# A two-layer diffusion backbone on one core: four weight tiles of layer 1's v placed in attention's operand slots, row statistics put off by two products, and another order of VectorE at the last scores

## The chip, the cores and the metric

The kernel runs on one core of a Trainium2 chip. The metric is the device time of one execution in microseconds. A run is given as the median of several executions. Besides, one execution is taken with the hardware profiler; it has its own time and a trace of every instruction.

A core has five engines with one instruction queue each: TensorE (PE in the profile, with its weight loads as PEld), VectorE (DVE), ScalarE (ACT), GpSimd (POOL) and SyncE (SP). An engine executes its queue in order. If an instruction waits, everything behind it on that engine waits too.

## The reference

The model has two layers over 512 latent tokens (x) and 256 context tokens (ctx), each 1024 wide. Layer 0 mixes tokens by retention with four heads. Layer 1 is a chunked gMLP; of it the part that the change touches is the projection to v and its normalisation over a row:

```
hx = rmsnorm(x, norm_g[i]) * (1 + scale_x) + shift_x
hc = rmsnorm(ctx, norm_g[i]) * (1 + scale_c) + shift_c

# layer 0, retention, per head: scores = (q @ k.T) * decay, o = scores @ v
o = o * lax.rsqrt(jnp.mean(o * o, axis=-1, keepdims=True) + NORM_EPS)
out_x = (o * silu(z)) @ w_out
x = x + gate_x * out_x

# layer 1, gMLP
u = h @ w_in[:, :2048]
v = h @ w_in[:, 2048:4096]
z = h @ w_in[:, 4096:]
v = v - mean(v)
v = v * rsqrt(mean(v * v) + NORM_EPS) * vnorm_g
mixed = w_s @ vg + b_s            # inside chunks of 128 tokens, 8 groups
y = u * mixed
x = x + gate_x * ((y * silu(z)) @ w_out)
return rmsnorm(x, final_g)
```

## The kernel before, in words

**Two halves of every number.** All data are 32-bit floats. Each operand of a product is kept as two halves: a high one, rounded to the type fp32r, and the low rest. `split` (L132) makes them: ScalarE copies the source into the high half (a cast), VectorE subtracts the high half from the source. `mm3` (L126) adds three matmuls for each term: low by high, high by low, high by high. So one weight tile costs one ScalarE cast and one VectorE subtraction, each 128 x 1024, and it waits for a free slot.

**Fewer products.** A large product of 2 by 2 blocks is done in seven products instead of eight, in the order `PAIRED` (L152): B11, B21, T1, T2, B22, T3, T4. The weight of a product whose name begins with B is one block of the matrix. That of a T product is a difference of two blocks (a raw sum: VectorE subtracts one 128 x 1024 raw block from another). `WITH` (L151) names the operand made of the tokens: A11 for B11, A12 for B21, S1 for T1, S2 for T2, S4 for B22, S3 for T3 and A22 for T4. `Product.run` (L369) runs one product of 24 matmuls into a bank of PSUM and then combines: `snap` (L350) is a ScalarE copy of the bank into SBUF, `plus` (L354) a VectorE addition of a bank to an earlier copy. There are eight PSUM banks, six with the tag ps and two with the tag tm. For a block of columns B21 uses a tm bank (y), and T1 takes another (z). T1 of the next block can start only when a plus has read such a bank to its end; T4 goes into the same bank x as B11, T2 and T3 after the plus of T3 in that block.

**The stream of weights.** `Stream` (L155) holds the list of all weight tiles in the order of their use. `pump` (L182) sends loads of raw blocks on SP's queue whenever a slot for a raw is free. `upto(n)` (L196) makes the tiles up to number n: it takes the raw sum if one is needed, takes a slot, and splits. At its end it makes the sum of the next tile ahead of its split. `sum(n)` (L214) does only the sum. `get(ahead=2)` (L239) returns the next tile and prepares two more behind it. The tiles lie in a ring of four slots, hl0 to hl3 (`hl_tile`, L110), unless an item names a slot of its own by `place_at` (L287). Layer 1's v has four blocks of columns, taken in two pairs: 0 and 1, then 2 and 3. For the first pair the item list (L290 to L297) puts the two tiles of B11 into oA22 and oS2; all others go to the ring.

**Attention.** The slots oA11, oA12, oA22 and oS1 to oS4 have 8 KB for each partition. While a head runs, its v lies in oA11, oS1 and oS2 (`load_v`, L903), z in oA12, and the transposed output og in oS3 and oS4; oA22 is free. `attend` (L962) has six steps, three for each half (hf) of the queries, and two further turns (LAG = 2). In a turn i, `score` (L973) issues the score products of step i, then VectorE multiplies by the decay (tile pf) and `split` gives ph on ScalarE and pl on VectorE. `pv` (L992) issues the products with v of step i - 2. After the last of a half, `finish` (L1005) normalises the rows: ScalarE squares and takes a square root, VectorE a reciprocal and two multiplications that give gt. `flip` (L1018) turns gt with eight transposes on TensorE and splits the result into og. Beside these, each turn takes pieces of other work off generators: qs and vs (loads and splits of the next head), wo (the weight tiles of this head's output product).

**Between the layers.** `project_out` (L1052) multiplies og with the output weights for each half of the tokens and four weight tiles (c), and adds the result to acc on VectorE (128 x 256 at a time). In the last head it calls hooks: `prepare` (L1192) at (hf, c) = (0, 2), which opens layer 1's loads and calls `Q.upto(Q.at + 1 + 2 + 2)`, and `first_half` (L1141) for each (hf, c). That starts the norm of layer 1 for the first half of the tokens: `by_tokens` (L1104) transposes acc and squares it on ScalarE, `inverse` (L1120) and `rms` (L1127) give the inverse root (tile sums, spread out by TensorE to rs), `scaled` (L1135) multiplies f by rs and scales it, `op` and `keep` (L320, L323) split the result into a slot. The second half of the tokens and the operands S1 to S4 and A22 are made in `second_half` (L1161), a generator, one piece after each of the first products of v.

**Layer 1's v.** The loop at L1215 to L1224 runs all products of a pair by name and block. `v1_done` (L1203) is called when a part of v is finished: two row statistics (bns, 128 x 256 each on VectorE, `bn_stats`), and a spill of v to DRAM by GpSimd's DMA queue. After both pairs the statistics are aggregated, and the loop over u, z and the output products follows.

**Who sets the order.** `Queue` (L38) wraps an engine. With `kept` an engine's instructions keep the order of the text; `fence()` (L47) keeps later instructions of that engine behind the last one issued so far, without a semaphore. Where neither is set, the tile scheduler orders the instructions of an engine within the dependences of tiles and slots. All rows of the profile say L54, because the wrapper issues every instruction there; rows are told apart by the program's names.

Of the kernel before, what the change touches and what calls it, by code (L numbers as in the profile page):

```python
# [18 lines left out]
HEADS = 4  # L19
# [7 lines left out]
HS = 256  # L27
# [40 lines left out]
def hybrid_kernel(ctx, tc, xT_d, cT_d, cv_d, sv_d, rows_d, ada0_d, adag_d, w_d, rope_d, dec_d, ws_d, id_d, out_d):  # L68
    nc = tc.nc
    pe, act, dve, sp = (Queue(tc, e) for e in (nc.tensor, nc.scalar, nc.vector, nc.sync))  # L70
# [11 lines left out]
    def st(shape, tag, dt=F32, bufs=1, name=None):  # L82
        return sb.tile(shape, dt, tag=tag, name=name or tag, bufs=bufs)
# [34 lines left out]
    def t2(name, shape=(P, 512), dt=F32):  # L118
        return st(list(shape), "t2", dt, bufs=T2, name=name)
# [124 lines left out]
    Q = Stream()  # L244
# [42 lines left out]
    def place_at(tag):  # L287
        return lambda: st([P, 2, 1024], tag, F32R, name="hl_e")

    V1_SLOTS = W + ["dec", "rope", "g0", "g2", "g3"]  # L290
    for a, b in ((0, 1), (2, 3)):
        for name in PAIRED:
            for cb in (a, b):
                Q.item(("v1", cb), name, place_at(("oA22", "oS2")[cb]) if (a, name) == (0, "B11") else None)
        for u in ("11", "21", "12", "22"):
            for cb in (a, b):
                Q.load((("v1", cb), u), V1_SLOTS, 2, parts_of(("v1", cb), u))  # L297

# [528 lines left out]
    def aside(work):  # L827

        act.pinned = dve.pinned = True
        r = next(work, None)  # L830
        act.pinned = dve.pinned = False
        return r
# [53 lines left out]
    wos = {}  # L886
# [75 lines left out]
    def attend(h, qs, vs):  # L962
        q, k, kc = qk.pop(h)
        v, z = vv.pop(h)
        dt = dts[h]
        og = [st([P, 2, 4, HS], tag, F32R, name="og") for tag in ("oS3", "oS4")]
        steps = [(hf, j) for hf in range(2) for j in range(0, NK, 2)]
        ph, po, pend = {}, {}, []

        def key(j):  # L970
            return (k[j // 2], j % 2) if j < NT else (kc, j - NT)

        def score(hf, j):  # L973

            p = pt(tag="tm")
            for o in range(2):
                src, jj = key(j + 1 - o)
                for m in range(2):
                    l = (src[:, 0, m, jj * P:jj * P + P], src[:, 1, m, jj * P:jj * P + P])
                    mm3(p[:, o * HS:o * HS + HS], l, (q[hf][:, 0, m, :], q[hf][:, 1, m, :]), m == 0, m == 1)  # L980
            j1 = j + 1
            s0 = hf * HS - P * j1 + P * (NT - 1) if j < NT else XW + hf * HS - P * (j1 - NT) + P * (NC_T - 1)
            base = dt[:, s0:s0 + HS]
            both = bass.AP(base.tensor, base.offset, [base.ap[0], (P, 2), (1, HS)])
            two = lambda x: x.rearrange("p (o t) -> p o t", o=2)
            a = t2("pf")
            dve.scalar_tensor_tensor(two(a), two(p), 1.0 / 16.0, both, ALU.mult, ALU.mult)
            hl = t2("ph", dt=F32R), t2("pl", dt=F32R)
            split(hl, a)
            ph[hf, j] = hl  # L990

        def pv(hf, j):  # L992
            if j == 0:
                po[hf] = [pt(), pt()]
            h, l = ph.pop((hf, j))
            src = v[j // 2]
            for jj in range(2):
                for t in range(2):
                    o = (1 - jj) * HS + t * P
                    mm3(po[hf][t], (h[:, o:o + P], l[:, o:o + P]), (src[:, 0, jj, :], src[:, 1, jj, :]),  # L1000
                        j + jj == 0, j + jj == NK - 1)
            if j == NK - 2:
                finish(hf)

        def finish(hf):  # L1005
            ss = st([P, 2], "ss", bufs=2)
            for t in range(2):
                act.activation(t2("junk"), po[hf][t], AF.Square, accum_out=ss[:, t:t + 1])
            act.activation(ss, ss, AF.Sqrt, bias=eps, scale=1.0 / 512)
            dve.reciprocal(ss, ss)  # L1010
            gts = []
            for t in range(2):
                g = t2("gt")
                dve.scalar_tensor_tensor(g, po[hf][t], ss[:, t:t + 1], z[:, 2 * hf + t, :], ALU.mult, ALU.mult)
                gts.append(g)
            pend.append((hf, gts))

        def flip():  # L1018
            hf, gts = pend.pop(0)
            for fp in range(2):  # L1020
                pq = pt()
                for b in range(2):
                    for t in range(2):
                        o = b * HS + t * P
                        pe.transpose(pq[:, o:o + P], gts[t][:, (2 * fp + b) * P:(2 * fp + b) * P + P], ident)
                src = pq.rearrange("p (b t) -> p b t", b=2)
                split((og[hf][:, 0, 2 * fp:2 * fp + 2, :], og[hf][:, 1, 2 * fp:2 * fp + 2, :]), src)

        LAG = 2
        wo = load_wo(h)  # L1030
        for i in range(len(steps) + LAG):
            if i < len(steps):
                score(*steps[i])
            if i >= LAG:
                pv(*steps[i - LAG])
            aside(qs)
            if i > 4:
                aside(vs)
            if i == len(steps):
                flip()  # L1040
            if (h, i) == (0, 2):
                sp.pinned = True
                for c in range(4):
                    load(acc[:, 2 * c:2 * c + 2, :], xT_d[:, 2 * c:2 * c + 2, :])
                sp.pinned = False
            if i < 5:
                aside(wo)
            if i in (3, 5, 6):
                step()
        return og, flip  # L1050

    def project_out(ws, og, flip, parts, then=None, between=None, prepare=None):  # L1052
        for hf in range(2):
            sl = slice(hf * HS, hf * HS + HS)
            for c in range(4):
                w = ws[c]
                if (hf, c) == (0, 2):
                    flip()
                    if prepare:
                        prepare()  # L1060
                for work in parts:
                    aside(work)
                if then is None and hf == 1 and c < 3:
                    step()
                if between:
                    between(hf, c)
                for mi in range(2):
                    m = 2 * c + mi
                    p = pt((P, HS))
                    for kk in range(4):  # L1070
                        o = kk * 256 + mi * P
                        mm3(p, (w[:, 0, o:o + P], w[:, 1, o:o + P]), (og[hf][:, 0, kk, :], og[hf][:, 1, kk, :]), kk == 0, kk == 3)
                    dve.scalar_tensor_tensor(acc[:, m, sl], p, gate0[:, m:m + 1], acc[:, m, sl], ALU.mult, ALU.add)
                    if then:
                        then(hf, m)
# [37 lines left out]
    def residual():  # L1113
        while flipped:
            i, pq = flipped.pop(0)
            xs = t2("xs")
            act.copy(xs, pq)
            spill(x1_d[i], xs)
# [73 lines left out]
    def prepare():  # L1192
        Q.stage = 2
        Q.free += V1_SLOTS[len(W):] + [w for w in W if w not in Q.free]
        Q.pump()
        Q.upto(Q.at + 1 + 2 + 2)

    project_out(wos.pop(HEADS - 1), og, flip, (), then=half_sum, between=first_half, prepare=prepare)


    bns = st([P, NT, 8, 6], "bns")

    def v1_done(cb):  # L1203
        def done(name, c):
            if name == "21":
                t = t2("snap")
                act.copy(t, c)
                c = t
            th, nh = int(name[0]) - 1, int(name[1]) - 1
            for t in range(2):  # L1210
                dve.bn_stats(bns[:, 2 * th + t, 2 * cb + nh, :], c[:, t * HS:t * HS + HS])
            spill(vt_d[2 * cb + nh][:, 2 * th:2 * th + 2, :], c.rearrange("p (t n) -> p t n", t=2))
        return done

    chain = second_half()  # L1215
    for a, b in ((0, 1), (2, 3)):
        prods = {q: Product(tokens, v1_done(q)) for q in (a, b)}
        for name in PAIRED:
            for q in (a, b):
                prods[q].run(name, Q.get())  # L1220
                if a == 0 and (q == 0 and name in ("B11", "B21", "T1", "T2", "B22") or (name, q) == ("B11", 1)):
                    next(chain)
            if (a, name) == (0, "B21"):
                residual()  # L1224
    bsb = st([P, D], "rope", name="bsb")
    load(bsb, rows_d[2:3, :].partition_broadcast(P))
    wsT = st([P, D], "dec", name="wsT")
# [265 lines left out]
```

## Time and profile before

| | |
|---|---|
| median of 3 runs | 893.61 us (890.0 to 894.43) |
| the profiled execution, its own time | 895.05 us |
| its span, from first to last instruction | 893.3 us |
| mean granted TensorE clock | 0.998 |
| VectorE: the splits of weight tiles (hl), 195 | 236.6 us, 1220 ns each |
| VectorE: raw sums, 92 | 111.7 us, 1219 ns each |
| ScalarE: casts of weight tiles, 195 | 203.8 us, 1051 ns each |
| DMA | 153.81 MB, mean 172 GB/s |

The profiled execution has 1.75 us around its span, and is 1.44 us above the median. Busy time counts an instruction from its start to its end, and for TensorE the ends are modelled, so neighbours can overlap: the time that TensorE loses is better read from the distance of two starts than from the busy share. In a row of the timeline the first number is the start in us from the span's start, the second the stretch that the group covers, then the engine, the line, the operation, the tiles it writes and reads, the shape and the number of instructions; in brackets stands the idle time before it and what ended that. A row of the waits gives engine, tile, the releaser, the total in us, how often, and the longest. A row of the windows gives a stretch, its length, the busy time of each engine with the number of instructions, the granted clock and the share of the DMA engines.

### The profile page before, as it was taken

The page shows a single profiled execution, that of the slowest core. Times are in us where ns is not written, and L with a number is a line of the kernel's source. Part 1 is how long each engine was busy: PE and PEld are TensorE (multiplying, and loading weights), DVE is VectorE, ACT ScalarE, POOL GpSimd, SP SyncE. Part 2 cuts the span into 40 slices and gives each one's busy share as a digit, 9 for nine tenths or more (in the row PEclk, how much of TensorE's full clock was granted, in tenths as well). Part 3 has the DMA queues.
Part 4 walks back from the last instruction along what each step waited for, and adds up shares of the span by engine and source line. Part 5 has one row for each costly group of instructions (what it writes and reads, how often), then busy time and mean ns, then how long its engine had stood idle before and what let it go on. Part 6 is the DMA issues. An engine that isn't in the chain of part 4 may idle for free.

```text
span 893.3 us, 16943 instructions
## 1 busy us (share of the span) xinstructions
PE 878.2 (98%) x6884; PEld 835.9 (94%) x6884; DVE 712.8 (80%) x996; ACT 461.9 (52%) x717; POOL 51.5 (6%) x88
## 2 busy tenths in 40 slices
PE   8999999999999999999999999989999999999997
PEld 6899999999999999998989999989999899899986
DVE  2689967699779876878677558999898578688995
ACT  5464644443545435636265449744666446356434
POOL 0001201002101101000000001010000000000000
PEclk9999999999999999999999999999999999999999
DMA  9933967457577458847354512455335135036112
GB/s 337 403 126 107 298 221 261 141 180 230 191 231 243 152 161 326 282 130 251 128 158 150 164 48 79 156 179 189 131 121 172 62 119 189 24 119 212 56 64 95
DMA packets 75486, 153.81 MB, mean 172 GB/s; under 512 B 7696, under 2 KB 34448, under 8 KB 75408
## 3 DMA queue, kind: packets, MB, share of 16 engines
q1 hardware_dynamic: 68544, 130.69, 44.8%
q0 software_dynamic: 6720, 22.03, 6.5%
q8 instruction: 54, 0.88, 0.4%
q14 instruction: 24, 0.20, 0.1%
q10 hardware_dynamic: 144, 0.01, 0.0%
HBM read 128.58 MB, written 24.12 MB: 171 GB/s over the span
## 4 chain that ended last, share of the span: by engine, by line
PE 86%; DVE 7%; ACT 3%; DMA 2%; issue 1%; SPq 1%; DVEq 0%; ACTq 0%
PE pst L54 86%; DVE hl L54 2%; DVE f L54 1%; DMA xq<-in_xT_dram 1%; DMA raw<-in_w_dram 1%; ACT junk L54 1%; DVE oS L54 1%; SPq L54 1%; DVE snap L54 0%; ACT hl L54 0%; DVE pf L54 0%; DVE pl L54 0%; DVE o L54 0%; DVE bns L54 0%; ACT L54 0%
## 5 line engine op out<-in xcount | busy, mean ns | idle before, releaser
L54 DVE TENSOR_TENSOR hl<-raw,hl 128x1024 fp32r<-128x1024 f32 x195 | 236.6, 1220 | 76.0 <-ACT hl L54 75.9
L54 ACT CAST hl<-raw 128x1024 fp32r<-128x1024 f32 x195 | 203.8, 1051 | 138.5 <-PE pst L54 63.4
L54 PE MATMUL pst<-hl,oS 128*128 128x256 f32 x1152 | 135.5, 278 | 0.0
L54 PEld LDWEIGHTS pst<-hl,oS 128*128 128x128 f32 x1152 | 134.0, 188 | 0.8 <-ACT snap L54 0.8
L54 PE MATMUL pst<-oS,hl 128*128 128x256 f32 x1104 | 133.3, 279 | 0.7 <-ACT oS L54 0.5
L54 PEld LDWEIGHTS pst<-oS,hl 128*128 128x128 f32 x1104 | 129.9, 188 | 2.3 <-ACT oS L54 1.0
L54 PE MATMUL pst<-oA,hl 128*128 128x256 f32 x936 | 117.2, 281 | 0.2
L54 PEld LDWEIGHTS pst<-oA,hl 128*128 128x128 f32 x936 | 111.8, 189 | 2.5 <-DVE rope_b L54 0.8
L54 DVE TENSOR_TENSOR raw<-raw 128x1024 f32<-128x1024 f32 x92 | 111.7, 1219 | 1.0 <-DMA raw<-in_w_dram 0.4
L54 ACT COPY snap<-pst 128x512 f32<-128x512 f32 x92 | 53.9, 586 | 102.1 <-PE pst L54 101.6
L54 PE MATMUL pst<-hl,oA 128*128 128x256 f32 x816 | 100.0, 282 | 2.7 <-DVE snap L54 2.7
L54 PEld LDWEIGHTS pst<-hl,oA 128*128 128x128 f32 x816 | 97.7, 191 | 2.9 <-issue 2.8
L54 PE MATMUL pst<-og,hl 128*128 128x256 f32 x768 | 92.5, 281 | 0.0
L54 PEld LDWEIGHTS pst<-og,hl 128*128 128x128 f32 x768 | 90.5, 189 | 1.0 <-issue 0.5
L54 PE MATMUL pst<-v,ph 128*128 128x512 f32 x192 | 60.1, 395 | 0.0
L54 PE MATMUL pst<-hl,ya 128*128 128x512 f32 (+1 forms) x246 | 59.2, 386 | 0.0
L54 PEld LDWEIGHTS pst<-hl,ya 128*128 128x128 f32 x246 | 45.3, 188 | 9.5
L54 DVE TENSOR_TENSOR snap<-pst,snap 128x512 f32<-128x512 f32 x69 | 47.2, 685 | 4.9 <-PE pst L54 4.6
L54 ACT CAST ph<-pf 128x512 fp32r<-128x512 f32 x24 | 14.9, 622 | 66.9 <-DVE pf L54 66.5
L54 PE MATMUL pst<-hl,hc 128*128 128x256 f32 x384 | 47.4, 280 | 0.0
L54 PEld LDWEIGHTS pst<-hl,hc 128*128 128x128 f32 x384 | 46.0, 189 | 0.0
L54 PEld LDWEIGHTS pst<-v,ph 128*128 128x128 f32 x192 | 36.2, 188 | 7.3
(177 smaller groups left out, 1001.1 us busy)
## 6 DMA issues: line engine op xcount, KB each, us to landing
raw<-in_w_dram SPq DMA_DIRECT2D x224, 256.0 KB, 4.1
bg<-in_adag_dram SPq DMA_DIRECT2D x32, 512.0 KB, 4.4
ada_w<-in_ada_dram SPq DMA_DIRECT2D x16, 512.0 KB, 9.1
raw<-in_w_dram SPq DMA_DIRECT2D x16, 512.0 KB, 4.2
bg<-in_dec_dram SPq DMA_DIRECT2D x12, 512.0 KB, 4.4
v<-snap POOLq DMA_DIRECT2D x16, 256.0 KB, 5.0
z<-snap POOLq DMA_DIRECT2D x16, 256.0 KB, 4.7
v<-v SPq DMA_DIRECT2D x8, 512.0 KB, 4.0
```

The costliest lines, as they stand in the source:

```text
L54: made = op(*args, **kw)
```

## The change

It has four parts.

1. The tiles of B11 for blocks 0 and 1 go to oS1 and oS2, and those of B21 to oA22 and oS3. Before, B11's went to oA22 and oS2, and B21's into the ring.
2. `prepare` makes the tiles of layer 1 up to B21's (`FIRST_V1 + 4`). A new hook `turned` calls `first_half` and, at (hf, c) = (1, 2) and (1, 3), makes the two tiles of T1 as well, which go into the ring. `get` makes two tiles ahead as before.
3. The row statistics of a finished part are put in a list and issued when more than two parts are waiting there, that is some products later; what is left is issued after the loop. The spill stays where it was. At T1 of block 1, the raw sums of items 12 and 13, the tiles of T4 for blocks 0 and 1, are issued early.
4. In `attend`, `finish` of the first half issues only ScalarE's squares and root; the reciprocal and the two multiplications (`gated`) wait in a list. In the next turn VectorE issues the score's pf first, then a fence, and the split's pl and `gated` come behind. In that turn and the one before, the pieces of other work are taken at another place of the text.

```
@@ -287,11 +287,13 @@
+    FIRST_V1 = len(Q.items)
     V1_SLOTS = W + ["dec", "rope", "g0", "g2", "g3"]
     for a, b in ((0, 1), (2, 3)):
         for name in PAIRED:
             for cb in (a, b):
-                Q.item(("v1", cb), name, place_at(("oA22", "oS2")[cb]) if (a, name) == (0, "B11") else None)
+                home = {"B11": ("oS1", "oS2"), "B21": ("oA22", "oS3")}.get(name) if a == 0 else None
+                Q.item(("v1", cb), name, place_at(home[cb]) if home else None)
@@ -965,7 +967,7 @@ attend
-        ph, po, pend = {}, {}, []
+        ph, po, pend, due = {}, {}, [], []
@@ -985,6 +987,8 @@ score
             dve.scalar_tensor_tensor(two(a), two(p), 1.0 / 16.0, both, ALU.mult, ALU.mult)
+            if due:
+                dve.fence()
             hl = t2("ph", dt=F32R), t2("pl", dt=F32R)
             split(hl, a)
@@ -1007,6 +1011,11 @@ finish
             act.activation(ss, ss, AF.Sqrt, bias=eps, scale=1.0 / 512)
+            due.append(lambda: gated(hf, ss))
+            if hf == 1:
+                due.pop(0)()
+
+        def gated(hf, ss):
             dve.reciprocal(ss, ss)
             gts = []
@@ -1031,8 +1040,14 @@ attend
             if i < len(steps):
                 score(*steps[i])
+            if due:
+                due.pop(0)()
+                aside(qs)
+                aside(wo)
             if i >= LAG:
                 pv(*steps[i - LAG])
+            if due:
+                continue
             aside(qs)
@@ -1193,9 +1208,14 @@ prepare
-        Q.upto(Q.at + 1 + 2 + 2)
-
-    project_out(wos.pop(HEADS - 1), og, flip, (), then=half_sum, between=first_half, prepare=prepare)
+        Q.upto(FIRST_V1 + 4)
+
+    def turned(hf, c):
+        first_half(hf, c)
+        if hf == 1 and c >= 2:
+            Q.upto(FIRST_V1 + 3 + c)
+
+    project_out(wos.pop(HEADS - 1), og, flip, (), then=half_sum, between=turned, prepare=prepare)
@@ -1207,21 +1227,34 @@ v1_done
-            for t in range(2):
-                dve.bn_stats(bns[:, 2 * th + t, 2 * cb + nh, :], c[:, t * HS:t * HS + HS])
+            stats.append((th, 2 * cb + nh, c))
             spill(vt_d[2 * cb + nh][:, 2 * th:2 * th + 2, :], c.rearrange("p (t n) -> p t n", t=2))
         return done
+
+    stats = []
+
+    def statistics(n):
+        while len(stats) > n:
+            th, cb, c = stats.pop(0)
+            for t in range(2):
+                dve.bn_stats(bns[:, 2 * th + t, cb, :], c[:, t * HS:t * HS + HS])
@@ the loop over v's products
             for q in (a, b):
-                prods[q].run(name, Q.get())
+                w = Q.get()
+                if (a, name, q) == (0, "T1", 1):
+                    for n in (12, 13):
+                        Q.sum(FIRST_V1 + n)
+                prods[q].run(name, w)
+                statistics(2)
                 if a == 0 and (q == 0 and name in ("B11", "B21", "T1", "T2", "B22") or (name, q) == ("B11", 1)):
                     next(chain)
             if (a, name) == (0, "B21"):
                 residual()
+    statistics(0)
```

## The prediction, made before the changed kernel ran

> **What bounds the kernel now.** I read the page first, then TensorE's waits, then its timeline at each wait, then VectorE's timeline at the same places.
>
> ```profile
> span 893.3 us, 16943 instructions
> PE 878.2 (98%) x6884; PEld 835.9 (94%) x6884; DVE 712.8 (80%) x996; ACT 461.9 (52%) x717; POOL 51.5 (6%) x88
> PE 86%; DVE 7%; ACT 3%; DMA 2%; issue 1%; SPq 1%; DVEq 0%; ACTq 0%
> ...
> PE pst L54 <- DVE snap L54: 2.7, 1, 2.7
> PE pst L54 <- DVE pl L54: 1.5, 3, 0.7
> ```
>
> TensorE is the bound: busy 98%, 86% of the chain that ended last. The change removes no matmul, so it can only close holes in TensorE's queue. The two waits on VectorE are such holes: one for a snap add, three for the low half of a score (pl). A hole's true size is read from starts, because the modelled ends overlap. First the three places where the transposes of gt precede the last products of a head (LAG puts them so), beside an undisturbed set of the same eight transposes:
>
> ```profile
> 364.12 1.03 PE L54 MATMUL pst<-ident,gt 128*128 128x128 f32 x8
> 365.48 0.50 PE L54 MATMUL pst<-v,pl 128*128 128x512 f32 x1 [0.33 <-DVE pl L54]
> ...
> 414.14 1.04 PE L54 MATMUL pst<-ident,gt 128*128 128x128 f32 x8
> 415.61 0.50 PE L54 MATMUL pst<-v,pl 128*128 128x512 f32 x1 [0.43 <-DVE pl L54]
> ...
> 465.38 1.03 PE L54 MATMUL pst<-ident,gt 128*128 128x128 f32 x8
> 467.13 0.51 PE L54 MATMUL pst<-v,pl 128*128 128x512 f32 x1 [0.71 <-DVE pl L54]
> ...
> 475.45 1.03 PE L54 MATMUL pst<-ident,gt 128*128 128x128 f32 x8
> 476.24 17.21 PE L54 MATMUL pst<-og,hl 128*128 128x256 f32 x144
> ```
>
> Undisturbed, the next work starts 0.79 us after the first transpose. Here it starts 1.36, 1.47 and 1.75 us after. The losses are 0.57, 0.68 and 0.96, together 2.2 us. The fourth head shows none.
>
> Second, the end of layer 1's first pair of v blocks. The names: B11, B21, T1, T2, B22, T3, T4 each run for blocks 0 and 1, 24 matmuls a product.
>
> ```profile
> 542.36 0.38 PE L54 MATMUL pst<-ident,acc 128*128 128x128 f32 x2
> 542.94 1.16 PE L54 MATMUL pst<-ident,acc 128*128 128x128 f32 x6 [0.19 <-DVE acc L54]
> 543.85 2.98 PE L54 MATMUL pst<-og,hl 128*128 128x256 f32 x24
> ...
> 553.29 0.70 PE L54 MATMUL pst<-ident,sums 128*128 128x128 f32 x4
> 553.75 5.70 PE L54 MATMUL pst<-hl,oA 128*128 128x256 f32 x48
> 559.29 21.92 PE L54 MATMUL pst<-hl,oS 128*128 128x256 f32 x192
> 583.88 6.29 PE L54 MATMUL pst<-hl,oA 128*128 128x256 f32 x39 [2.67 <-DVE snap L54]
> ...
> 601.90 2.32 PE L54 MATMUL pst<-hl,oS 128*128 128x256 f32 x19
> ```
>
> 192 matmuls are eight products: 2.74 us each. T4 of block 0 starts at 583.88 after 2.67 us of nothing. The second pair's T1 (first with oS1 again) starts at 601.90: six products later, which at 2.74 would be 16.4 us; it took 18.0. The clock tells where the other 1.6 us went:
>
> ```profile
> 581.00:584.00 3.00, 0.34 (x3) 0.17 (x3) 3.00 (x6) 1.88 (x2) 0.05 (x1) 1.00 0.80 255
> 584.00:585.00 1.00, 1.00 (x10) 1.00 (x11) 1.00 (x4) 0.21 (x1) 0.92 (x2) 1.00 0.89 279
> 586.00:587.00 1.00, 1.00 (x6) 1.00 (x6) 1.00 (x4) 0.00 (x0) 0.00 (x0) 0.50 0.87 311
> 587.00:588.00 1.00, 1.00 (x6) 1.00 (x6) 0.90 (x1) 0.00 (x0) 0.00 (x0) 0.50 1.01 393
> ```
>
> The columns after the stretch are its length, the busy time of PE, PEld, DVE, ACT and POOL, then PEclk. Two microseconds after the hole TensorE gets half its clock, and runs 6 matmuls a microsecond where it ran 10. So the hole costs 2.7 + 1.6 us. [...]
>
> **The change, part by part.**
>
> *Last scores first.* In the scheduled order VectorE now has, at the last score of each head, pf, (reciprocal), pl, and only then gt. Before, pf stood behind the reciprocal, which waits for ScalarE's square root:
>
> ```profile
> 461.04 0.17 DVE L54 RECIPROCAL ss<-ss 128x2 f32<-128x2 f32 x1 [2.30 <-ACT ss L54]
> 461.24 1.41 DVE L54 SCALAR_TENSOR_TENSOR gt<-pst,ss,z 128x512 f32<-128x512 f32 x2
> ...
> 464.30 0.68 DVE L54 SCALAR_TENSOR_TENSOR pf<-pst,dt 128x512 f32<-128x512 f32 x1
> ...
> 466.39 0.68 DVE L54 TENSOR_TENSOR pl<-pf,ph 128x512 fp32r<-128x512 f32 x1
> ```
>
> ```profile
> L54 ACT CAST ph<-pf 128x512 fp32r<-128x512 f32 x24 | 14.9, 622 | 66.9 <-DVE pf L54 66.5
> ```
>
> pf falls into those idle 2.30 us. ScalarE casts ph right after the square root, 0.62 us by its group; pl ends near 462.4 instead of 467.1, four microseconds before it is wanted. What is late next is gt: 1.41 us behind pl gives 463.8, wanted by the transposes at 465.38; 1.5 us are left. The same sums hold in the other heads. The skipped asides are made up in the next turn, so no work is added. Gain: 2.2 us. Bounds: 0 if something else ends at the same moment, 2.2.
>
> *Four tiles in attention's slots.* The tiles of B11 and B21 go to oS1, oS2, oA22 and oS3 instead of two there and two in the ring of four. The ring is free sooner, so T1's two splits move before the stage, and the work behind them moves up. No instruction is added. The waits that are added: the cast into oS1 waits on ScalarE for the last product that reads v's second tile, and ahead of it nothing but behind it stand the two og casts for the output product. By the order of ScalarE they come some 0.6 us later than before; VectorE's og halves with them end about 0.6 us before TensorE wants them. The cast into oS3 waits until the first half of the output product is through, and behind it stand the squares of acc: 0.1 us, covered by 24 matmuls. Cost 0; from 0 to 0.5 us if the cover is thinner.
>
> *What VectorE's queue gives.* These are its rows at both ends and the price of each kind:
>
> ```profile
> 542.40 1.65 DVE L54 SCALAR_TENSOR_TENSOR acc<-pst,gate,acc 128x256 f32<-128x256 f32 x4
> 543.97 0.47 DVE L54 SCALAR_TENSOR_TENSOR f<-acc,gs,f 128x256 f32<-128x256 f32 x1
> ...
> 554.43 1.23 DVE L54 TENSOR_TENSOR f<-f,rs 128x1024 f32<-128x1024 f32 x1
> ...
> 579.53 0.68 DVE L54 TENSOR_TENSOR snap<-pst,snap 128x512 f32<-128x512 f32 x1
> 580.13 1.21 DVE L54 TENSOR_TENSOR hl<-raw,hl 128x1024 fp32r<-128x1024 f32 x1
> 581.26 0.74 DVE L54 BATCH_NORM_STATS2 bns<-snap 128x6 f32<-128x256 f32 x2
> 581.93 1.20 DVE L54 TENSOR_TENSOR raw<-raw 128x1024 f32<-128x1024 f32 x1
> 583.05 1.28 DVE L54 TENSOR_TENSOR snap<-pst,snap 128x512 f32<-128x512 f32 x2
> ```
>
> Start to start: snap 0.60, a 1024-wide split 1.13, a pair of bns 0.67, a raw sum 1.12, a 256-wide step about 0.4.
>
> Step 1. acc of the transposes at 542.36: two of the four acc now run before it, because no ring split stands in front. The transposes need 0.79 again instead of 1.49: TensorE is 0.7 us earlier.
>
> Step 2. VectorE then goes without pause to f times rs: one A11 and one A12 split, three ring splits, three raw sums, six 256-wide steps and three tiny ones: 2 x 1.13 + 3 x 1.13 + 3 x 1.12 + 6 x 0.4 + 0.3 = 11.7 us. It starts at 543.2 (0.8 earlier than the row at 543.97), so f times rs comes at 554.9, half a microsecond later than now. TensorE meets two new holes of about 0.4 and 0.9 us: at the transposes of sums (the reciprocal stands behind a raw sum) and at T1 of block 0, whose bank is freed by an add that comes 4.5 us after f times rs (two splits, four 256-wide steps and the add: 2.26 + 1.6 + 0.6). T1 starts at 559.5 instead of 559.29: step 1's gain is used up.
>
> Step 3. From f times rs to T4 took 583.88 - 554.43 = 29.45 us. In the new order that stretch has one split less (T2's two went ahead, T4's second came in), one raw sum less and one pair of bns less: 1.13 + 1.12 + 0.67 = 2.92. T4 can start at 554.9 + 26.5 = 581.4. TensorE itself is there at 559.5 + 8 x 2.74 = 581.4. The hole is gone, 2.5 us earlier, and with it the half clock.
>
> Step 4. The bns put off come later. From there to the add that frees T1's bank in the second pair VectorE has six splits, five raw sums, five pairs of bns and two adds: 6.8 + 5.6 + 3.35 + 1.2 = 16.95, that is 598.3; TensorE alone would be there at 597.8. So T1 starts at 598.3 against 601.90, 3.6 us earlier, the next one 3.5. After that VectorE gains room as it does now.
>
> The weights of layer 1's u are now requested ahead of v's last ones on SP's queue; those have over 10 us until their sums. Cost 0.
>
> Sum: 2.2 + 3.5 = 5.7 us. Span 893.3 becomes 887.6; the profiled execution's 895.05 becomes 889.35. That execution is 1.4 above the median of the runs shown, 893.61; less 5.7 this is 887.9. I say 888.0.
>
> **Rivals.**
>
> *The hole moves* (25%). If steps 2 and 4 are worse by a microsecond each, VectorE is the bound from T1 to T1 and 2 of the 3.5 are lost: gain 3.7, 889.9. For it: VectorE has no pause there now. Against: 2.9 us of work did move ahead.
>
> *The half clock has another cause* (7%) and stays. TensorE would lose 1.6 between T4 and T1, of which VectorE's bound at 598.3 hides 0.5: gain 4.6, 889.0.
>
> *Everything closes* (13%). No new holes in step 2: 0.7 us more in front, and up to 1 us in step 4. Gain 7.4, 886.2.
>
> *Slower* (4%). A cast that waits in ScalarE's queue holds all behind it; one does so now:
>
> ```profile
> 464.16 1.06 ACT L54 CAST hl_e<-raw 128x1024 fp32r<-128x1024 f32 x1 [1.69 <-DMA raw<-in_w_dram]
> ```
>
> In the new order the cast into oS1 stands before og. Beyond its cover of 0.6 us each microsecond is TensorE's, and from about 2 us the clock halves as it did after 2.67: 1.6 more. It must be 4.7 us late to eat the gain (4.7 - 0.6 + 1.6 = 5.7), and 9.1 to give 898.1, 0.5% slower. Nothing in the rows makes it wait longer than for its product.
>
> *The change does not act* (5%): the order is met but the waits stay; 893.
>
> **How the numbers follow.** The forecast has 46%. 0.5% is 4.5 us, which is about what a measurement of this kernel can tell from no change; the runs shown spread over 4.4. Faster by more: the forecast, everything, and about half of the second rival: 62%. Within: most of the first rival, the rest of the second, the fifth: 34%. Slower: 4%. Range: the first rival's 889.9 and everything's 886.2, each widened by 1.5 for the spread of a median: 884.7 to 891.6.
>
> **What would show it.** Right: no wait for pl and none for snap in TensorE's waits; PEclk 1.00 from 560 to 620; pf right after a head's last score; small holes, under 1 us, at sums and T1. Wrong: a hole over 2 us near 558 or 596; og casts that TensorE waits for; a stretch of half clock.

## The result, and the profile after

The changed kernel takes 888.82 us in the median of 13 runs (888.38 to 891.14); the kernel before takes 893.34 us in 13 runs beside it (889.68 to 895.34). The medians lie 4.5 us apart. The comparison of the runs, which is not the quotient of the medians, gives the ratio 0.996, 3.6 us less, with a 95% interval of 0.9947 to 0.9973: 2.4 to 4.7 us less. The profiled execution took 888.54 us; its span is 886.8 us, 6.5 shorter than that of before.

The page of the changed kernel with the chain by engine, and below it one row of TensorE's waits (releaser, total in us, times, longest):

```profile
span 886.8 us, 16946 instructions
PE 876.3 (99%) x6884; PEld 835.0 (94%) x6884; DVE 712.5 (80%) x996; ACT 461.5 (52%) x717; POOL 51.5 (6%) x88
...
PE 91%; DVE 4%; ACT 3%; DMA 1%; issue 1%; SPq 0%; DVEq 0%
```

```profile
PE pst L54 <- DVE snap L54: 0.6, 2, 0.4
```

No row for pl is left among the waits, and snap's 2.7 has become 0.6 in two pieces. No engine does less work: VectorE is busy 712.5 us instead of 712.8. TensorE's share of the chain rises from 86% to 91%.

TensorE's timeline at the places that the prediction showed of before:

```profile
363.30 1.03 PE L54 MATMUL pst<-ident,gt 128*128 128x128 f32 x8
364.09 0.47 PE L54 MATMUL pst<-v,pl 128*128 128x512 f32 x1
...
412.70 1.03 PE L54 MATMUL pst<-ident,gt 128*128 128x128 f32 x8
413.50 0.48 PE L54 MATMUL pst<-v,pl 128*128 128x512 f32 x1
...
463.09 1.03 PE L54 MATMUL pst<-ident,gt 128*128 128x128 f32 x8
463.88 0.48 PE L54 MATMUL pst<-v,pl 128*128 128x512 f32 x1
...
539.08 1.04 PE L54 MATMUL pst<-ident,acc 128*128 128x128 f32 x8
539.88 3.07 PE L54 MATMUL pst<-og,hl 128*128 128x256 f32 x24
...
549.44 0.71 PE L54 MATMUL pst<-ident,sums 128*128 128x128 f32 x4
549.90 6.00 PE L54 MATMUL pst<-hl_e,oA 128*128 128x256 f32 x48
556.16 22.05 PE L54 MATMUL pst<-hl,oS 128*128 128x256 f32 x192 [0.26 <-DVE snap L54]
578.22 16.59 PE L54 MATMUL pst<-hl,oA 128*128 128x256 f32 x144
595.17 5.04 PE L54 MATMUL pst<-hl,oS 128*128 128x256 f32 x41 [0.36 <-DVE snap L54]
```

Each set of transposes is now followed after 0.79 us, the undisturbed distance. T4 (578.22) comes without a wait. The distance of these starts from those of before is a running account, in us:

```
                                        before   after    ahead by   step
first head's transposes of gt           364.12   363.30     0.82
work behind the third head's            467.13   463.88     3.25     +2.43
work behind the transposes of acc       543.85   539.88     3.97     +0.72
work behind the transposes of sums      553.75   549.90     3.85     -0.12
T1 of block 0                           559.29   556.16     3.13     -0.72
T4 of block 0                           583.88   578.22     5.66     +2.53
T1 of block 2                           601.90   595.17     6.73     +1.07
end of the span                         893.3    886.8      6.5      -0.2
```

The first 0.82 us stand ahead of every place that was changed, so they are a difference between two executions (at 230 us the changed kernel is 1.0 us ahead already); the last part on the hardware says which. Of the 2.43 us, 2.21 are the three waits for pl; the other 0.2 lies in the products between the heads.

What moved is seen on VectorE. Here are the same 35 us of TensorE's work in both kernels (stretch, its length, busy time of PE, PEld, DVE, ACT, POOL), first of before, then of after, 3.25 us earlier:

```profile
505.00:515.00 10.00, 10.00 (x55) 8.58 (x54) 5.83 (x8) 5.24 (x10) 0.00 (x0) 1.00 0.87 269
515.00:525.00 10.00, 10.00 (x75) 9.26 (x74) 5.98 (x11) 3.88 (x9) 0.00 (x0) 1.00 0.26 83
525.00:540.00 15.00, 14.75 (x129) 14.51 (x128) 8.93 (x15) 8.09 (x21) 2.18 (x4) 1.00 0.15 54
```

```profile
501.75:511.75 10.00, 10.00 (x55) 8.58 (x54) 7.12 (x10) 5.34 (x10) 0.00 (x0) 1.00 0.82 263
511.75:521.75 10.00, 10.00 (x74) 9.26 (x74) 8.37 (x13) 4.53 (x9) 0.00 (x0) 1.00 0.24 79
521.75:536.75 15.00, 14.75 (x129) 14.51 (x127) 10.69 (x17) 9.55 (x23) 2.17 (x4) 1.00 0.19 71
```

VectorE does 26.18 us of work there instead of 20.74. Most of these 5.4 us are splits and raw sums of v's first tiles (four instructions more, of 1.22 us each), which before stood in the crowded stretch behind. From f times rs to T4 that stretch has no pause of more than 0.1 us on VectorE in either kernel; it only begins with less to do.

### The profile page after: what moved, and what is told of

It reads as the page before. It is cut to its first block, busy times and chain, and to the rows that moved or that the text cites. A ratio compares the mean times of both kernels' runs of the same rounds, so it can differ in the third digit from the quotient of the medians.

```text
span 886.8 us, 16946 instructions
## 1 busy us (share of the span) xinstructions
PE 876.3 (99%) x6884; PEld 835.0 (94%) x6884; DVE 712.5 (80%) x996; ACT 461.5 (52%) x717; POOL 51.5 (6%) x88
## 4 chain that ended last, share of the span: by engine, by line
PE 91%; DVE 4%; ACT 3%; DMA 1%; issue 1%; SPq 0%; DVEq 0%
PE pst L54 91%; DVE hl L54 1%; DMA xq<-in_xT_dram 1%; ACT f L54 1%; ACT junk L54 1%; DVE raw L54 1%; SPq L54 0%; DVE f L54 0%; ACT hl L54 0%; ACT oA L54 0%; DVE o L54 0%; ACT xs L54 0%; DVE oS L54 0%; DVE xq L54 0%; DVE bns L54 0%
## 5 line engine op out<-in xcount | busy, mean ns | idle before, releaser
L54 ACT CAST hl<-raw 128x1024 fp32r<-128x1024 f32 x193 | 201.7, 1050 | 141.7 <-PE pst L54 66.3
L54 PE MATMUL pst<-hl,oA 128*128 128x256 f32 x768 | 92.2, 278 | 0.0
L54 PEld LDWEIGHTS pst<-hl,oA 128*128 128x128 f32 x768 | 90.0, 188 | 0.2 <-issue 0.2
```

What stands on the lines that cost most here:

```text
L54: made = op(*args, **kw)
```

## The experiments

A time of one chip is compared with the kernel before on the same chip, by the ratio.

**The parts apart.** One kernel has only the new `attend`, the other all but that.

```
scores_alone: before.py with attend() of the change
v_alone:      the changed kernel with attend() of before
```

> Only the new order at the last scores, everything else as before. Theory: the three waits for pl go, 0.57 + 0.68 + 0.96 = 2.2 us, and the hole ahead of T4 stays at 2.7: about 891.1 us. Rival: a part of the 2.2 us is lost again in the next stage, because VectorE is later there: 892 or more.

Measured: ratio 0.9974 (0.9965 to 0.9983), that is 2.3 us less. The three losses ahead of pl are gone from the trace. The hole at T4 stays, but its row reads differently:

```profile
556.99 22.77 PE L54 MATMUL pst<-hl,oS 128*128 128x256 f32 x192
581.38 17.20 PE L54 MATMUL pst<-hl,oA 128*128 128x256 f32 x144 [1.62 <-DVE snap L54]
598.42 1.81 PE L54 MATMUL pst<-hl,oS 128*128 128x256 f32 x14
```

The 192 matmuls ahead took 22.77 us where before's took 21.92, so TensorE came later to the same add on VectorE and waited 1.6 instead of 2.7 us. Behind it the clock stayed full, and T1 came 17.04 us after T4 instead of 18.02.

> Only the slots, the earlier tiles and the statistics put off, attention as before. Theory: the hole ahead of T4 goes with the half clock, 3.5 us: about 889.8 us, with the three waits for pl still there. Rival: half the executions of the kernel before have no half clock, and the part is worth 1.9 to 2.7 us in the median: 890.6 to 891.4.

Measured: ratio 0.9962 (0.9949 to 0.9975), 3.4 us less. The interval is 2.2 to 4.6 us, so the time alone does not decide between the theory's 3.5 and the rival's 1.9 to 2.7. In its trace T4 and T1 come with the same steps as in the changed kernel (+2.53, +1.07). Of the waits for pl only two are named there; by the starts the three heads lose 0.58, 0.92 and 0.25 us, so these losses too differ between executions. The two parts together, 2.3 + 3.4, make the 5.7 of the prediction; the changed kernel itself has 0.996 and, in a second series below, 0.9943: 3.6 and 5.1 us. The times do not show more closely that the parts add up.

**The kernel before, once more.**

> The kernel before, unchanged, profiled once more. Theory: the hole of 2.67 us ahead of T4 of block 0 comes every time, since it is VectorE's order that makes it; 893.3 us. The half clock behind it cost 1.6 us in the profiled execution, and that execution was 1.7 us above the median of all: if the half clock depends on where the hole falls against something that runs free of the kernel, this profile may show the hole with full clock behind it, and the second T1 then starts about 16.5 us behind T4 instead of 18.0; the times of the executions then scatter over at least 1.6 us. Rival: the half clock follows every such hole; then it stands in this profile too, 3.4 us long, and the 1.2 us by which the medians differ less than the two profiles come from elsewhere.

Measured: 894.19 us, ratio 1.0001 (0.999 to 1.0011). The hole of 2.67 us is there again, but now the clock is halved for 6.83 us, two stretches of 3.41, and from 0.6 us before the hole's end on (581.21). The windows that follow are cut at whole stretches of 3.413 us from the start of full clock. So long is the halved stretch in the first profile of before (585.34 to 588.75); the stretches of full clock on its two sides last 580.27 and 303.79 us, 170 and 89 times 3.4133, and that of the changed kernel's profile 877.22 us, 257 times 3.4133. They begin 5.07 us behind the span's start in before and 7.20 in the changed kernel. PEclk is the number after the five engines:

```profile
577.79:581.21 3.42, 1.37 (x13) 1.18 (x11) 3.42 (x6) 1.86 (x3) 0.54 (x1) 1.00 0.80 263
581.21:584.62 3.41, 2.79 (x13) 2.82 (x14) 3.41 (x7) 0.95 (x1) 1.08 (x2) 0.50 0.93 290
584.62:588.03 3.41, 3.41 (x18) 3.41 (x18) 1.32 (x3) 0.70 (x2) 0.00 (x0) 0.50 0.84 251
588.03:591.45 3.42, 3.42 (x32) 3.42 (x32) 3.29 (x6) 1.81 (x3) 0.64 (x2) 1.00 0.37 131
```

T1 came 19.32 us after T4, 1.3 us later than in the first profile of before. So the same hole costs 2.7 us and then 1.6 or 2.9 us for the clock. No profile shows it with full clock behind it (the hole of scores_alone was only 1.62 us long), but the granted clocks of all executions, under *The sum* below, say that this happens. The rival, one fixed stretch behind every such hole, falls.

**A hole of other lengths.** In `Product.plus`, for T3 of v's block 0 alone, with n = 4, 8 and 12:

```
             t = self.s.pop(key)
+            if name == "22" and not late22:
+                late22.append(name)
+                for _ in range(n):
+                    dve.tensor_scalar(t, t, 1.0, None, ALU.mult)
```

> The changed kernel with four extra multiplications by 1.0 on VectorE (128 x 512, about 0.35 us each by a 1024-wide row of 0.66) ahead of the add that frees T4's bank in block 0. Both theories: TensorE gets a hole of 1.0 to 1.4 us before T4, the clock stays full, and the time rises by about 1.3 us, since VectorE is the bound up to the second T1 as well: about 890.1.

> The same with eight multiplications: a hole of about 2.6 us, as long as that of the kernel before. Theory: the clock is judged in stretches of 3.41 us that run free of the kernel, so the same hole gives one halved stretch, two or none, by where it falls; the halved time is a multiple of 3.41 us here and starts at a boundary that has nothing to do with the hole's end. Rival: a hole of this length always halves the clock for one stretch that begins a fixed time after the hole, as in the first profile of before (1.5 us after).

> The same with twelve: a hole of about 4 us, longer than one stretch of 3.41. Both theories: the clock is halved. Theory: for 3.4 or 6.8 us, and its start may lie inside the hole. Rival: for 3.4 us, beginning 1.5 us after the hole's end.

Measured, one execution each: 890.82, 896.42 and 899.5 us, with holes of 1.36, 4.36 and 9.41 us. The last two were longer than meant: a multiplication takes 0.33 us, but the scheduler put splits and statistics between them; so no hole of before's length was made. The windows of hole4, then hole8, then hole12, cut as above:

```profile
576.71:580.12 3.41, 2.05 (x19) 1.88 (x18) 3.41 (x7) 1.04 (x1) 0.41 (x1) 1.00 0.52 169
580.12:583.53 3.41, 3.41 (x32) 3.41 (x31) 3.41 (x7) 0.87 (x2) 0.67 (x2) 1.00 0.82 296
```

```profile
580.14:583.55 3.41, 0.00 (x0) 0.00 (x0) 3.41 (x8) 0.28 (x1) 0.54 (x1) 1.00 0.76 231
583.55:586.96 3.41, 3.26 (x15) 3.29 (x16) 3.41 (x6) 0.00 (x0) 0.54 (x1) 0.50 0.20 77
586.96:590.38 3.42, 3.42 (x31) 3.42 (x30) 3.31 (x5) 1.53 (x2) 0.54 (x1) 1.00 0.07 22
```

```profile
581.78:585.19 3.41, 0.00 (x0) 0.00 (x0) 3.41 (x7) 0.00 (x0) 0.00 (x0) 0.50 0.32 124
585.19:588.61 3.42, 0.55 (x2) 0.58 (x3) 3.42 (x7) 0.00 (x0) 0.40 (x1) 0.50 0.00 0
588.61:592.02 3.41, 3.41 (x18) 3.41 (x17) 3.36 (x5) 0.00 (x0) 0.14 (x1) 0.50 0.20 77
```

In both longer holes the half clock begins inside the hole (T4 starts at 583.70 and 588.06), not 1.5 us behind it as the rival has it. In hole12 it lasts three windows, one more than was said. In these windows the work of one goes with the clock of the next. The same cut of the first profile of before has this:

```profile
581.92:585.34 3.42, 1.46 (x13) 1.49 (x14) 3.42 (x7) 1.42 (x2) 1.08 (x2) 1.00 0.86 265
585.34:588.75 3.41, 3.41 (x19) 3.41 (x18) 2.60 (x5) 0.66 (x2) 0.00 (x0) 0.50 0.97 315
```

A busy time at half clock counts as half here: 2.79 us of it were followed by half clock, 2.05 us at full clock by full. Then windows with 0, 0.28 (0.55 at half clock), 1.37, 1.40 (2.79 at half) and 1.46 us of work are followed by half clock, windows with 1.63 (3.26 at half), 1.71 and 2.05 us by full clock. Near the end of the first profile of before a window with 1.48 us (885.71 to 889.12) was still followed by full clock. In these windows the edge lies near 1.5 us of work in 3.41, less than half, as far as modelled ends allow; a window need not be empty, since 1.46 us of work did not keep the clock. By this edge, as an estimate, a hole of 2.67 us is enough if some 1.95 us of it (3.41 less 1.46) fall into one window, and not if it is shared out more evenly; the second case stands in no profile.

**Which half of the v part pays?** Three kernels, all with the new `attend`:

```
no_putoff          - if (a, name, q) == (0, "T1", 1): ... Q.sum(FIRST_V1 + n)
                   - statistics(2)
                   + statistics(0)

slots_and_scores   the same, and
                   - project_out(..., between=turned, prepare=prepare)
                   + project_out(..., between=first_half, prepare=prepare)
                   - Q.upto(FIRST_V1 + 4)
                   + Q.upto(FIRST_V1 + 2)

putoff_and_scores  - home = {"B11": ("oS1", "oS2"), "B21": ("oA22", "oS3")}.get(name) if a == 0 else None
                   + home = {"B11": ("oA22", "oS2")}.get(name) if a == 0 else None
                   - project_out(..., between=turned, prepare=prepare)
                   + project_out(..., between=first_half, prepare=prepare)
```

> The changed kernel with the row statistics at once again, and without the two early raw sums. Theory by the changed order: up to the add that frees T1's bank in the second pair VectorE has the same eight pairs of statistics, the same splits and the same sums, only in another order; so the hole of 0.5 us there stays, T4 comes without a hole, and the time is that of the changed kernel within 0.4 us: 888.8. Rival: the statistics put off are what closes the hole ahead of T4; then it comes back with at least the 0.67 us of one pair, and the time is 889.5 or more.

Measured: ratio 0.9949 (0.9937 to 0.9962), 4.6 us less than before, like the changed kernel (889.82 us on a chip where before took 894.56). The theory holds for T4: no wait ahead of it. The hole of 0.5 us at the second T1 that was to stay does not show: from soon after the first T1 on TensorE's products ran at 117.8 ns instead of 113.3 in this execution, so TensorE came later (the two rates are in the last part).

> The changed kernel once more, beside the next two on one chip. All theories: 888.8 us, 0.996 of the kernel before, no wait for snap over 0.6 us.

Measured: 888.95 us, ratio 0.9943 (0.9922 to 0.9965), the waits as expected. Its profiled execution took 885.31 us; the reason is below.

> The four slots and the new order at the last scores; without the hook that makes T1's tiles ahead, the statistics at once, the two raw sums where they were. Theory (VectorE's sum of work up to the add decides, and the scheduler brings T1's splits ahead by itself once the ring is free): up to the add that frees T4's bank there are one pair of statistics more and one split less than in the changed kernel, and up to T1's add the same; so no hole before T4 and 888.8 us, within 0.4. Rival (the parts add up, each closing its share of the 2.67 us): a hole of 1 us or more before T4, 890 or more.

Measured: 890.1 us, ratio 0.9959 (0.9942 to 0.9976). In the trace T4 follows without a wait:

```profile
556.73 22.89 PE L54 MATMUL pst<-hl,oS 128*128 128x256 f32 x192 [0.24 <-DVE snap L54]
579.45 17.12 PE L54 MATMUL pst<-hl,oA 128*128 128x256 f32 x144
596.41 3.81 PE L54 MATMUL pst<-hl,oS 128*128 128x256 f32 x31
```

As in no_putoff, the 192 matmuls ran at 117.8 ns (22.72 us from T1 to T4), which could hide a hole of 0.9 us. It hides none: the add that frees T4's bank ends at 578.08, 21.35 us behind T1's start, and at 113.3 ns TensorE would need 21.75; A22 is split by 575.10. So of the v part the four slots alone close the hole. The hook and the larger `upto` change almost nothing (against no_putoff one split of VectorE stands at another place up to f times rs), because the scheduler takes T1's splits ahead by itself as soon as the ring is free. The time misses the forecast by 0.9 us and lies where the rival had it, but without the rival's hole; 0.66 us of it are those 192 matmuls, 22.72 us instead of the 22.06 of the changed kernel's profile. The median is 1.15 us above the neighbour's, and the intervals overlap; whether the statistics put off are worth a part of that stays open.

> The reverse: the tiles of B11 in oA22 and oS2 and those of B21 in the ring, as before; statistics put off by two parts, the two raw sums early, the new order at the last scores. Theory by VectorE's order: the transposes of acc lose their 0.7 us again, but T1's two splits then stand behind, and f times rs comes as early as in the changed kernel; from there to the add that frees T4's bank stand two pairs of statistics and one split less than before, 2.5 of the 2.67 us; T4 comes after a hole of at most 0.3 us and the time is 888.9 to 889.3. The two remedies would then be worth the same 3.5 us each and no more together. Rival: without the slots the hole stays at 2 us or more and the half clock with it, 891.0 or more.

Measured: 890.16 us, ratio 0.9968 (0.9956 to 0.9981), 0.9 to 1.3 us over the forecast and under the rival's 891.0. Both missed. The transposes of acc lose 0.7 us as said. At T4:

```profile
556.98 22.10 PE L54 MATMUL pst<-hl,oS 128*128 128x256 f32 x192
580.80 16.61 PE L54 MATMUL pst<-hl,oA 128*128 128x256 f32 x144 [1.72 <-DVE oA L54]
597.25 3.00 PE L54 MATMUL pst<-hl,oS 128*128 128x256 f32 x25
```

```profile
578.27 0.69 DVE L54 TENSOR_TENSOR snap<-pst,snap 128x512 f32<-128x512 f32 x1
578.87 0.75 DVE L54 BATCH_NORM_STATS2 bns<-snap 128x6 f32<-128x256 f32 x2
579.53 1.21 DVE L54 TENSOR_TENSOR oA<-f,oA 128x1024 fp32r<-128x1024 f32 x1
```

The add that frees the bank is in time, as the count said. But T4 needs its operand A22 too, and in this order its split stands behind the add and a pair of statistics: TensorE waits 1.7 us for oA. The count looked at the bank alone. The clock stays full (granted clock 1.0 over the whole execution), and T1 comes 16.45 us later, so some of the loss is made up: from the first T1 to the second it takes 40.27 us, against 42.61 in before and 39.01 in the changed kernel. Putting off the statistics without the slots is a remedy for a part of the hole; the slots close it alone; together the two closed no more of it than the slots.

**One step further.** `statistics(2)` becomes `statistics(4)`.

> The changed kernel with the row statistics put off by four finished parts instead of two. Theory: one pair of statistics, 0.67 us, moves behind the add that frees T1's bank in the second pair; the hole of 0.5 us there goes, and the time is 0.5 us lower, about 888.3, less than the medians can tell; the trace shows the wait for snap at T1 of the second pair gone. Rival: the snaps held longer make ScalarE wait for a free tile, and a new wait for snap or for the operands stands somewhere in the second pair: 889 or more.

Measured: 889.16 us, ratio 0.9953 (0.9941 to 0.9964). The wait ahead of the second T1 is gone:

```profile
557.18 22.05 PE L54 MATMUL pst<-hl,oS 128*128 128x256 f32 x192 [0.27 <-DVE snap L54]
579.08 16.48 PE L54 MATMUL pst<-hl,oA 128*128 128x256 f32 x144
595.41 4.83 PE L54 MATMUL pst<-hl,oS 128*128 128x256 f32 x39
```

From T4 to T1 it takes 16.33 us instead of 16.95. That is 0.6 us where the theory had 0.5, and no new wait came; in the median it can't be seen. No version was measured to be faster than the changed kernel.

**TensorE's rate** (see the last part). In `Product.run`, once, ahead of the first product of all:

```
+            if nudged:
+                nudged.pop()
+                mm(bank[:, :P], ones, ones, start=True, stop=True, skip_group_check=True)
```

> The changed kernel with one more matmul, 128 x 128 of ones, into the bank of the very first product just before that product clears it; nothing else. In the profiles so far a product of layer 0 and 1 runs at one of two rates, 113.3 or 117.8 ns a matmul, steady over up to 100 us; from 60 to 158 us eight profiles of ten looked at ran at 117.8, and the one execution of the changed kernel that ran there at 113.3 took 885.3 us instead of 888.8. Theory: which rate comes is settled where the operands change, by how one matmul meets the next weight load; the extra matmul stands at that place ahead of the long stretch and changes the odds: 113.3 there in most executions and a median near 885.5. Rival: the rate is set by something outside TensorE's queue, such as the memory; the extra matmul changes nothing and the median is 888.9 again.

The count in this expectation was off: of the 13 profiles taken by then, 12 ran at 117.8 there. Measured: 889.18 us, ratio 0.9953 (0.9939 to 0.9966), and 117.8 ns from 60 to 158 us. The theory falls: one more matmul at that place doesn't set the rate.

## Why the prediction was right, point by point

- *Last scores first, 2.2 us.* In the trace each set of transposes is followed after 0.79 us instead of 1.36, 1.47 and 1.75, so the three losses of 2.2 us are gone; the times of that part alone gave 2.3. The order came as worked out; here is the third head on VectorE:

```profile
457.79 0.69 DVE L54 SCALAR_TENSOR_TENSOR pf<-pst,dt 128x512 f32<-128x512 f32 x1 [1.51 <-PE pst L54]
458.75 0.17 DVE L54 RECIPROCAL ss<-ss 128x2 f32<-128x2 f32 x1 [0.26 <-ACT ss L54]
459.25 0.69 DVE L54 TENSOR_TENSOR pl<-pf,ph 128x512 fp32r<-128x512 f32 x1 [0.34 <-ACT ph L54]
459.86 1.41 DVE L54 SCALAR_TENSOR_TENSOR gt<-pst,ss,z 128x512 f32<-128x512 f32 x2
```

  gt ends at 461.3, 1.8 us ahead of its transposes at 463.09; the prediction had 1.5.
- *Step 1, 0.7 us at the transposes of acc:* +0.72.
- *Step 2, two small new holes that use up step 1's gain:* the steps are -0.12 and -0.72. What VectorE does came as worked out: f times rs starts at 551.57, which in before's times (3.25 later) is 554.8 (predicted 554.9), and T1 at 559.4 (predicted 559.5). The two holes of 0.4 and 0.9 do not fit that start, which leaves 0.9 for both together; the steps make 0.84. One of them did not come: the next product follows the transposes of sums after 0.46 us in both kernels, and 0.1 of the 0.12 lies in the 24 matmuls of og ahead of them, which took 2.91 us instead of 2.81. At T1 the wait is 0.26 us, and about 0.3 of the 0.72 are the 48 matmuls of B21, which now run more slowly (see the last part); the prediction has no term for that. Here it costs nothing, because VectorE's add sets T1's start.
- *Step 3, T4's hole gone, 2.5 us:* +2.53. The sum was right, and the changed order has one split, one raw sum and one pair of statistics less in that stretch, as counted. But not all of that was needed. The experiments show that beside the four slots the hook, the early sums and the statistics put off add nothing to T4's start that the trace shows: the work was moved into VectorE's idle time by the free ring and the scheduler.
- *Step 4, a further 1.1 us to the second T1, with VectorE the bound there:* +1.07, with a wait of 0.36 for snap.
- *The added waits, 0 us:* TensorE waits nowhere for og, so the rival that ended slower didn't come about.
- *The sum.* From the third head's end to T1 the trace gives 6.73 - 3.25 = 3.48 (predicted 3.5), and with the heads 5.7. The medians gave 4.5, and 888.82 instead of 888.0; the ratio gave 3.6, and its interval does not reach 5.7. The 62% for more than 4.5 us are thus not borne out. The step that was mis-sized is the last one, where the whole 5.7 was taken off a median: the 1.6 us of half clock belong to one profiled execution. The mean granted clock is known of 76 executions of the kernel before and 19 of the changed one, and one halved stretch of 3.41 us in 892 lowers it by 0.0019. Of the 76, 20 have 0.999 or 1.0 and so had no such stretch at T4; 35 have 0.997 or less, as none of the 19 has. Their medians are 892.8 and 894.15 us. The mean clock is 0.9978 before and 0.9984 after: on average the half clock costs about 0.6 us, not 1.6, and 4.7 would have been the gain to expect. (The upper end of the range, 889.9 + 1.5, is 891.4 and not 891.6; nothing hangs on it.)
- *The rivals.* The half clock went with the hole and didn't stay. *Slower* let the clock halve from a hole of about 2 us on: of the holes at T4, those of 1.36, 1.62 and 1.72 us had full clock behind them (hole4, scores_alone, putoff_and_scores), those of 2.67, 4.36 and 9.41 had half clock (both profiles of before, hole8, hole12), and none lies between. The hole moved only as far as 0.36 + 0.26 us. By the times alone *the hole moves*, with its gain of 3.7, would fit the ratio's 3.6 better than the forecast; the trace speaks against it. From the first T1 to the second it takes 39.01 us, 0.65 more than fourteen products at 2.74, where that rival loses 2.

## What to carry to other kernels

Where a busy engine delays TensorE, look for its idle time some tens of microseconds ahead, and for the slot that keeps work from moving there; a scheduler may do the rest. Two remedies for one hole did not add up here: test each alone. Against one profiled execution a sum can be right to 0.1 us a step and still be a microsecond off the median, so take a second profile of the kernel before, see which losses come back, and look at the granted clock of every execution before a loss to the clock is put into a forecast.

## What the runs showed of the hardware

**Steady rates.** At full granted clock nearly all of TensorE's products in the profiles of before and of the changed kernel run at one of two steady rates, 113.3 or 117.8 ns from one 256-wide matmul to the next. In both the rate changes only where the work changes. It differs between executions of one kernel. The same 192 matmuls in two executions of the changed kernel, first the profiled one, then the one of the second series:

```profile
82.29 22.78 PE L54 MATMUL pst<-hl,oS 128*128 128x256 f32 x192
```

```profile
81.86 21.92 PE L54 MATMUL pst<-hl,oS 128*128 128x256 f32 x192
```

From 60 to 158 us this is worth 3.4 us, as much as lies between 888.54 and 885.31 and 0.2 more. The 0.82 us by which the first head of the changed kernel was ahead come from the same: from 190 to 230 us its products ran at 113.3 and those of before at 117.8, and for some 15 us ahead of that it was the other way round. What sets the rate stays open; the extra matmul of the last experiment changed nothing.

A third rate comes with the products whose weight tile lies in one of attention's slots (hl_e): 120 ns in the profiles of before and of the changed kernel, and rows of the same length in five other traces (24 matmuls in 3.04 or 3.11 us, 48 in 5.99 or 6.00). In the kernel before these are the two of B11, in the changed kernel those of B21 as well: their 48 matmuls take 6.00 us where they took 5.70, with tiles of the ring, in the first profile of before. The reason was not tested.

**The clock.** The edge near 1.5 us of work in a window of 3.41 (1.46 us were followed by half clock, 1.48 by full), and the half clock that began inside a hole (0.15 us ahead of T4's start in hole8, 6.28 in hole12), were not expected; the prediction had read the half clock as following the hole's end.
